# A two-layer hybrid encoder step on one core: the HGRN2 products inside chunks put into one step per group, and a convolution without its zero columns

## The chip, the core and the metric

The program runs on one NeuronCore of one Trainium2 chip. A core has TensorE (PE in the profile; its weight loads are listed apart as PEld), VectorE (DVE), ScalarE (ACT), GpSimd (POOL) and SyncE (SP), which here only issues DMAs. Each engine takes its instructions in the order in which they were written; the engines wait for one another by semaphores. The metric is the device time of one launch in microseconds: the median over runs, 2416.27 us for the kernel before (three runs, 2414.19 to 2416.79).

## The reference

Each of two layers computes `x + W_out . concat[mLSTM | retention | SSD | HGRN2](RMSNorm(x) W_in)` for 1024 prompt frames and 8 streams of 16 frames, 1152 tokens in all, in float32. Two mixers matter here. HGRN2 is a recurrence with a forget decay of its own for every key channel; inside a chunk the score of query t and key s has the decay between them in it, channel by channel:

```python
def hgrn_block(s_prev, xs):
    q, k, v, lf = xs
    b = jnp.cumsum(lf, axis=2)
    diff = b[:, :, :, None, :] - b[:, :, None, :, :]
    w = jnp.exp(jnp.where(causal_tril(l)[:, :, None], diff, -jnp.inf))
    s = jnp.einsum("bhtk,bhsk,bhtsk->bhts", q, k, w)
    o = jnp.einsum("bhts,bhsv->bhtv", s, v) + jnp.einsum("bhtk,bhkv->bhtv", q * jnp.exp(b), s_prev)
    bl = b[:, :, -1]
    s_new = jnp.exp(bl)[..., None] * s_prev + jnp.einsum("bhsk,bhsv->bhkv", k * jnp.exp(bl[:, :, None, :] - b), v)
    return s_new, o
```

The SSD branch begins with a causal depthwise convolution of four taps over the frames (`up = concat([buf, u])`, with a `buf` of three rows that is zero for the prompt), then SiLU. The mLSTM mixer multiplies queries and keys of two heads at a time, masked by head.

## The kernel before

**Work units.** Both layers go through the list `ORDER`: HGRN2 head 0, retention pair 0, SSD half 0, mLSTM pair 0, then h1, r1, s1, m1, h2, h3. A unit has a *projection* (columns of W_in against all 1152 normalised tokens) and a *mixer* (the recurrence). After the units of a layer come two halves of the output projection. The projection is float32 work made of three passes (high part times high part, and each high part times the other's low part), in `slab_run`: lines 404 to 406 where a run gives features on the partitions ("fm": 128 weight columns are held, 384 tokens streamed) and lines 425 to 427 where it gives tokens on the partitions ("tm": 128 tokens are held, 256 weight columns streamed). Three such matmuls, for one of eight blocks of 128 inputs, are called a *k-step* here.

**Interleaving.** `merge` writes the projection of a unit and the mixer of the unit before it into one stream: after each k-step it lets the mixer generator run until its next `yield` (a *step*) when `j * np_ * pace < i * nm_`, where i counts k-steps, j steps, `np_` is the number of k-steps and `nm_` the declared number of steps. So the steps are spread evenly: a mixer with fewer steps has longer ones. A retention projection has 216 k-steps, an HGRN2 projection 120 (72 in its first run, `ev_vg`, and 48 in its second, `ev_qf`). Beside h3's projection runs h2's mixer, of which the last six steps are carried into the output projection (`CARRY`). `self.after(1, f)` runs f at the start of the next step; `self.later(n, f)` runs it n half-chunks of the projection later (`tick`).

**An HGRN2 mixer (`unit_h`, lines 1419 to 1760).** 1152 tokens are nine chunks of 128 in three groups of three. Scores inside a chunk are built from blocks of 4 tokens (`base`, line 1555) and five *levels* of halves of 64, 32, 16, 8 and 4 tokens. `level` makes for each level a tile X of decayed keys and queries: two subtractions on DVE, an exponential on ACT, then, one step later, a product on POOL and one on DVE. `pick` multiplies the halves of X on PE: line 1573 for the three small levels (12 matmuls each with 32-column weights; the profile counts 24 instructions, since a float32 matmul is issued twice), line 1585 for the two large ones (6 matmuls of 32 columns, 3 of 64). Each of base and the five picks has a step of its own and a PSUM tile of its own, evicted in the next step by DVE (`copy_predicated` under a mask, or a copy) or ACT. Level X is made three steps ahead (`LOOK`), and the first two levels of the first group stand in the mixer's opening steps. `prep` makes the decayed keys K and queries Q for the state, `keys` transposes K (line 1605), `state` multiplies K and values (line 1624), `out` forms the outputs (lines 1663, 1665), `post` normalises them (line 1683) and `fin` transposes them back (line 1692). Projection results come in through `ev_qf`; at the next tick `fours` rescales q and k. A mixer has 31 steps for h0 and h1, 29 for h2 and h3.

**Convolution (`unit_s`, `conv`).** A tile of 3 + 384 columns holds the channel's frames; for the first group POOL writes zeros into the three columns ahead (line 1179), and three `scalar_tensor_tensor` operations on DVE (line 1197) add the taps.

**mLSTM (`unit_m`).** At its start the mixer loads decay rows (`load_e`, `load_wi`), multiplies them with the queries on POOL (`use_wi`), then masks the queries by head on POOL (`Z`, through `by_head`), which line 833 multiplies.

Of the kernel before, what the change touches and what calls it, by code (L numbers as in the profile page):

```python
# [120 lines left out]
class Kernel:  # L121
# [609 lines left out]
    def unit_m(self, l, p):  # L731
# [38 lines left out]
        def mix():  # L770
# [175 lines left out]

            load_e(0)
            load_wi(0)
            use_wi(0)
            Z(0)  # L950
# [197 lines left out]
    def unit_s(self, l, u):  # L1148
# [22 lines left out]
        def conv(a, g, ps):  # L1171
# [19 lines left out]
            areas = [(o[:, 0:np_], lambda w: t[:, w:w + np_])]  # L1191
            if g == 2:
                areas.append((o[:, 256:384].rearrange("p (n t) -> p n t", t=16), lambda w: sv[:, :, w:w + 16]))

            def taps(w):
                for oo, src in areas:
                    nc.vector.scalar_tensor_tensor(out=oo, in0=src(w), scalar=cw(w), in1=oo, op0=ALU.mult, op1=ALU.add)
# [221 lines left out]
    def unit_h(self, l, h):  # L1419
# [3 lines left out]
        def ev_qf(m, g, ps):  # L1423
# [30 lines left out]
            self.later(1, lambda: fours(g))  # L1454

# [40 lines left out]
        def mix():  # L1496
            hw = self.vB[:, 40 + 4 * l + h:40 + 4 * l + h + 1]
            stt = {}
            LOOK = 3
# [6 lines left out]

            def level(W, g, li):
                hs = 64 >> li
                w = G3 if (g < 2 or hs <= 8) else 256
                X = self.f()  # L1510
                W["X"][li] = X, w
                xv = lambda a: a[:, 0:w].rearrange("p (n e t) -> p n e t", e=2, t=hs)
                ref = xv(b[g])[:, :, 0, hs - 1:hs].to_broadcast([128, w // (2 * hs), hs])
                self.tt(xv(X)[:, :, 0], ref, xv(b[g])[:, :, 0], ALU.subtract)
                self.tt(xv(X)[:, :, 1], xv(b[g])[:, :, 1], ref, ALU.subtract)
                self.act(X[:, 0:w], X[:, 0:w], AF.Exp)

                def mults():
                    self.tt(xv(X)[:, :, 0], xv(X)[:, :, 0], xv(k[g])[:, :, 0], ALU.mult, "p")
                    self.tt(xv(X)[:, :, 1], xv(X)[:, :, 1], xv(q[g])[:, :, 1], ALU.mult)  # L1520

                self.after(1, mults)
# [24 lines left out]
            def base(g, W):  # L1547


                sc = self.ps("sc")  # L1550
                for c in range(3):
                    for j in range(4):
                        rs = slice(32 * j, 32 * j + 32)
                        ts = slice(128 * c + 32 * j, 128 * c + 32 * j + 32)
                        nc.tensor.matmul(sc[rs, 32 * c:32 * c + 32], k[g][:, ts], q[g][:, ts], start=True, stop=True)
# [3 lines left out]
                self.after(1, lambda: nc.vector.copy_predicated(D, self.lev[:, LEVW - 96:], sc[:, 0:96]))  # L1559

            def pick(g, W, li):
                hs = 64 >> li
                x, w = W["X"].pop(li)
                n = w // 128
                sc = self.ps("sc")
                half = lambda a: a.rearrange("p (n e t) -> p n e t", e=2, t=hs)[:, :, 1]
                if li >= 2:
                    D = W["D"]
                    for c in range(n):
                        for j in range(4):  # L1570
                            rs = slice(32 * j, 32 * j + 32)
                            xt = x[:, 128 * c + 32 * j:128 * c + 32 * j + 32]
                            nc.tensor.matmul(sc[rs, 16 * c:16 * c + 16].rearrange("p (n t) -> p n t", t=hs), xt, half(xt),
                                             start=True, stop=True)
                    cp = lambda a: a.rearrange("p (n t) -> p n t", t=hs)
                    mk = self.lev[:, 48 * (li - 2):48 * (li - 2) + 16 * n]
# [445 lines left out]
```

## Time and profile before

| what | value |
|---|---|
| median of three runs | 2416.27 us |
| the profiled execution | 2415.16 us, its span 2413.4 us |
| PE busy | 2333.9 us (97%), weight loads 2258.8 us |
| DVE, ACT, POOL busy | 1390.7, 1076.4, 976.2 us |
| mean granted TensorE clock | 0.988 |
| DMA | 204.06 MB, mean 85 GB/s |

The span runs from the program's first instruction to its last; 1.8 us of the execution lie outside it. Busy is the time in which an engine has at least one instruction in work. The matmuls overlap, each lasting longer than the distance to the next, so PE's cost is read from the distances between starts. The profile gives the granted clock as a share of full speed (1.00 is 2.4 GHz, 0.50 is 1.2 GHz).

### The profile page before, as it was taken

To read this page: it belongs to the slowest core of one execution; us is meant where nothing else is said; L and a number is where in the kernel's file an instruction comes from. 1 tells how busy PE (TensorE), PEld (TensorE's weight loads), DVE (VectorE), ACT (ScalarE), POOL (GpSimd) and SP (SyncE) were. 2 spreads that over 40 slices of the span, in tenths; PEclk is the share of its full clock that TensorE was granted. 3 is DMA by queue.
4 is the path that set the end of the run, shared out by engine and by line. 5 is a ranking of instruction groups with operands and counts; after the bars stand their busy time and mean duration, and the time that the engine had idled before them with its cause. 6 is when DMAs were issued, how large, how long until landed. Compare 5 with 4: busy or idle time off the path is not lost.

```text
span 2413.4 us, 49607 instructions
## 1 busy us (share of the span) xinstructions
PE 2333.9 (97%) x18992; PEld 2258.8 (94%) x18992; DVE 1390.7 (58%) x3419; ACT 1076.4 (45%) x2780; POOL 976.2 (40%) x1179
## 2 busy tenths in 40 slices
PE   7999999999999998999989999999999999999998
PEld 7999999999999998899988999999899999888998
DVE  4756753773765376544368376537737654666443
ACT  6344563434455345433243445634344653454332
POOL 2443344353334335423135334432633452345353
PEclk9999999999999999999989999999999999999999
DMA  5111233221123222536411212323111333225552
GB/s 151 37 49 45 81 91 77 65 60 52 50 83 95 61 72 74 158 114 213 133 37 37 61 54 80 90 65 77 49 48 55 98 78 81 50 85 167 159 170 82
DMA packets 273736, 204.06 MB, mean 85 GB/s; under 512 B 57908, under 2 KB 264140, under 8 KB 273500
## 3 DMA queue, kind: packets, MB, share of 16 engines
q1 hardware_dynamic: 273180, 200.81, 29.2%
q8 instruction: 150, 2.46, 0.4%
q14 instruction: 86, 0.70, 0.1%
q0 software_dynamic: 320, 0.09, 0.0%
HBM read 148.53 MB, written 52.29 MB: 83 GB/s over the span
## 4 chain that ended last, share of the span: by engine, by line
PE 83%; DVE 8%; ACT 3%; issue 2%; DMA 1%; POOL 1%; SPq 1%; DVEq 0%; ACTq 0%; POOLq 0%
PE w L425 11%; PE w L404 11%; PE w L427 11%; PE w L426 11%; PE w L406 11%; PE w L405 11%; DVE f L212 3%; ACT f L215 2%; PE w L1310 1%; SPq L218 1%; DVE c L212 1%; PE w L1624 1%; PE w L1663 1%; PE w L1061 1%; PE w L833 1%
## 5 line engine op out<-in xcount | busy, mean ns | idle before, releaser
L425 PE MATMUL w<-hi,hnh 128*128 128x256 f32 (+1 forms) x2592 | 775.8, 299 | 0.0
L427 PE MATMUL w<-hi,hnl 128*128 128x256 f32 (+1 forms) x2592 | 731.9, 282 | 1.6 <-DVE hnl L492 1.6
L426 PE MATMUL w<-lo,hnh 128*128 128x256 f32 (+1 forms) x2592 | 731.7, 282 | 0.1
L425 PEld LDWEIGHTS w<-hi,hnh 128*128 128x128 f32 x2592 | 493.0, 190 | 6.1 <-issue 1.1
L426 PEld LDWEIGHTS w<-lo,hnh 128*128 128x128 f32 x2592 | 493.1, 190 | 3.5 <-issue 0.3
L427 PEld LDWEIGHTS w<-hi,hnl 128*128 128x128 f32 x2592 | 492.5, 190 | 2.2 <-DVE hnl L492 2.0
L215 ACT ACTIVATE f<-f 128x384 f32<-128x384 f32 (+1 forms) x475 | 244.1, 516 | 434.8 <-DVE f L212 275.0
L215 ACT ACTIVATE c<-c 128x512 f32<-128x512 f32 (+3 forms) x398 | 211.3, 534 | 292.4 <-DVE c L546 205.4
L212 POOL TENSOR_TENSOR f<-f,f 128x384 f32<-128x384 f32 (+2 forms) x268 | 226.7, 854 | 283.3 <-ACT f L215 210.3
L404 PE MATMUL w<-hnh,hi 128*128 128x384 f32 x960 | 339.3, 353 | 0.0
L212 POOL TENSOR_TENSOR lo<-raw,hi 128x512 fp32r<-128x512 f32 x148 | 195.0, 1318 | 332.3 <-ACT hi L202 279.2
L406 PE MATMUL w<-hnh,lo 128*128 128x384 f32 x960 | 324.6, 338 | 0.0
L405 PE MATMUL w<-hnl,hi 128*128 128x384 f32 x960 | 324.3, 338 | 0.0
L404 PE MATMUL w<-mxh,hi 128*128 128x384 f32 x768 | 268.7, 350 | 0.0
L406 PE MATMUL w<-mxh,lo 128*128 128x384 f32 x768 | 261.1, 340 | 0.0
L405 PE MATMUL w<-mxl,hi 128*128 128x384 f32 x768 | 260.9, 340 | 0.0
L212 POOL TENSOR_TENSOR c<-c,c 128x512 f32<-128x512 f32 (+2 forms) x120 | 128.9, 1083 | 221.2 <-ACT c L215 175.6
L212 DVE TENSOR_TENSOR lo<-raw,hi 128x512 fp32r<-128x512 f32 x140 | 114.4, 817 | 134.4 <-ACT hi L202 134.2
L404 PEld LDWEIGHTS w<-hnh,hi 128*128 128x128 f32 x960 | 181.6, 189 | 3.0 <-issue 1.8
L405 PEld LDWEIGHTS w<-hnl,hi 128*128 128x128 f32 x960 | 181.8, 189 | 0.8
L406 PEld LDWEIGHTS w<-hnh,lo 128*128 128x128 f32 x960 | 181.0, 189 | 0.0
L212 DVE TENSOR_TENSOR c<-c,w 128x384 f32<-128x384 f32 (+1 forms) x124 | 73.3, 595 | 184.8 <-PE w L406 121.6
(304 smaller groups left out, 3979.3 us busy)
## 6 DMA issues: line engine op xcount, KB each, us to landing
raw<-in_w_in SPq DMA_DIRECT2D x224, 128.0 KB
raw<-in_w_in SPq DMA_DIRECT2D x112, 256.0 KB
c<-mixd SPq DMA_DIRECT2D x96, 192.0 KB
raw<-in_w_out SPq DMA_DIRECT2D x64, 256.0 KB
xd<-c SPq DMA_DIRECT2D x66, 192.0 KB
mixd<-c SPq DMA_DIRECT2D x48, 256.0 KB
c<-xd SPq DMA_DIRECT2D x60, 192.0 KB
c<-sscr SPq DMA_DIRECT2D x36, 256.0 KB
```

Of the source, the lines that this page charges most:

```text
L212: (self.nc.vector if e == "v" else self.nc.gpsimd).tensor_tensor(out=out, in0=a, in1=b, op=op)
L215: self.nc.scalar.activation(out=out, in_=in_, func=func, scale=scale, bias=bias, **k)
L218: (e or self.nc.sync).dma_start(out=out, in_=in_)
L404: nc.tensor.matmul(o, hi[:, k, ms], xhi[:, k, :], start=(k == 0), stop=False)
L405: nc.tensor.matmul(o, hi[:, k, ms], xlo[:, k, :], start=False, stop=False)
L406: nc.tensor.matmul(o, lo[:, k, ms], xhi[:, k, :], start=False, stop=(k == KT - 1))
L425: nc.tensor.matmul(o, xhi[:, k, ts], hi[:, k, :w], start=(k == 0), stop=False)
L426: nc.tensor.matmul(o, xhi[:, k, ts], lo[:, k, :w], start=False, stop=False)
L427: nc.tensor.matmul(o, xlo[:, k, ts], hi[:, k, :w], start=False, stop=(k == KT - 1))
L833: nc.tensor.matmul(sc[:, 0:256], k[g][:, cs], qz.pop(c), start=True, stop=True)
L1061: nc.tensor.matmul(po[h], w[:, h], v[j][:, i, h], start=(c in (0, 8)), stop=(c == 0 or (c < 8 and h == 1)))
L1310: nc.tensor.matmul(po[:, 64 * h:64 * h + 64], pt[:, h], x_[:, 64 * h:64 * h + 64], start=True, stop=True)
```

## The change

**HGRN2.** The step functions `base` and `pick` are gone. `gram` issues all 57 products of a group in one step: 12 of base, 36 of the small levels, then 6 and 3 of the two large ones, into two PSUM tiles. One step later `evac` evicts all of them and builds the diagonal blocks (`diag`). `level` has moved out of the mixer. The first group's five levels are put off with `later` from `ev_qf`, so that they stand beside the unit's own projection; the levels of group g + 1 stand in the first three of the five steps of group g, `prep(g + 1)` in the third, `fresh(g + 1)` (the two POOL memsets) in the fourth. The mixer has 24 steps for every head: one opening step (`prep` and `fresh` of the first group), fifteen, and eight at the end. No DMA is added or taken away.

**Convolution.** The memset is gone; for the first group each tap covers only the columns that exist.

**mLSTM.** `Z(0)` stands ahead of `load_e(0)`, `load_wi(0)` and `use_wi(0)`.

```diff
@@ unit_m, mix
+            Z(0)
             load_e(0)
             load_wi(0)
             use_wi(0)
-            Z(0)
@@ unit_s, conv
-            if g == 0:
-                nc.gpsimd.memset(t[:, 0:3], 0.0)
-            else:
+            if g > 0:
...
+            if g == 0:
+                areas = [((lambda w: o[:, 3 - w:np_]), lambda w: t[:, 3:w + np_])]
@@ unit_h, ev_qf
             self.later(1, lambda: fours(g))
+            if g == 0:
+                for li in range(NLEV):
+                    self.later(2 + li, lambda li=li: level(Ws[0], 0, li, self.later))
@@ unit_h, mix
+            def gram(g, W):
+                sc, sb = self.ps("sc"), self.ps("sc")
+                mm = lambda o, a, b_: nc.tensor.matmul(o, a, b_, start=True, stop=True)
+                at = lambda li: 96 + 48 * (li - 2)
+                for c in range(3):
+                    for j in range(4):
+                        ts = slice(128 * c + 32 * j, 128 * c + 32 * j + 32)
+                        mm(sc[32 * j:32 * j + 32, 32 * c:32 * c + 32], k[g][:, ts], q[g][:, ts])
+                for li in range(2, NLEV):
+                    hs = 64 >> li
+                    x, w = W["X"].pop(li)
+                    for c in range(n):
+                        for j in range(4):
+                            xt = x[:, 128 * c + 32 * j:128 * c + 32 * j + 32]
+                            o = sc[32 * j:32 * j + 32, at(li) + 16 * c:at(li) + 16 * c + 16]
+                            mm(o.rearrange("p (n t) -> p n t", t=hs), xt, half(xt, hs))
+                for li in (1, 0):
...
+                            mm(sb[64 * j:64 * j + hs, 192 * li + hs * c:192 * li + hs * c + hs], xt[:, 0:hs], xt[:, hs:2 * hs])
+                def evac():
+                    nc.vector.copy_predicated(D, self.lev[:, LEVW - 96:], sc[:, 0:96])
...
+                    diag(W)
+                self.after(1, evac)
...
+            prep(0, Ws[0])
+            fresh(Ws[0])
+            yield
             for g in range(NG):
...
+                for s in range(5):
+                    if s == 0:
+                        gram(g, W)
+                        if V:
+                            out(g - 1, V, 0)
+                    elif s == 1:
                         keys(g, W)
+                        if V:
+                            out(g - 1, V, 1)
+                            out(g - 1, V, 2)
+                    elif s == 2 and V:
+                        post(g - 1, V)
+                    elif s == 3:
                         state(g, W)
...
+                    elif s == 4 and V:
+                        fin(g - 1, V)
+                    if g + 1 < NG:
+                        for li in ((0, 1), (2, 3), (4,), (), ())[s]:
+                            level(Ws[g + 1], g + 1, li, self.after)
+                        if s == 2:
+                            prep(g + 1, Ws[g + 1])
+                        if s == 3:
+                            fresh(Ws[g + 1])
                     yield
-        ... steps=31 if h < 2 else 29 ...
+        ... steps=24 ...
```

On PE, the first group of the first HGRN2 unit of layer 0 stood in the kernel before in six places with projection matmuls between them; four of the six are shown (w is a PSUM tile, f a tile of 384 columns, hi and lo weights, hnh and hnl tokens; sizes are those of the result, partitions by columns).

```order
L427 MATMUL w_1185<-hi_794,hnl_232 128x256
L1555 MATMUL w_1195<-f_792,f_827 32x32 x12
L425 MATMUL w_1185<-hi_794,hnh_231 128x256
...
L427 MATMUL w_1185<-hi_794,hnl_232 128x256
L1585 MATMUL w_1264<-f_1098 64x64 x3
L425 MATMUL w_1185<-hi_794,hnh_231 128x256
...
L1585 MATMUL w_1309<-f_1134 32x32 x6
L1605 MATMUL w_1320<-cst,f_1213 128x128 x3
L425 MATMUL w_1302<-hi_794,hnh_301 128x256
...
L1573 MATMUL w_1351<-f_1218 32x16 x12
```

Now the same products stand in one piece:

```order
L427 MATMUL w_1064<-hi_794,hnl_159 128x256
L1562 MATMUL w_1122<-f_792,f_827 32x32 x12
L1562 MATMUL w_1122<-f_907 32x16 x12
L1562 MATMUL w_1122<-f_943 32x16 x12
L1562 MATMUL w_1122<-f_984 32x16 x12
L1562 MATMUL w_1123<-f_888 32x32 x6
L1562 MATMUL w_1123<-f_866 64x64 x3
L425 MATMUL w_1064<-hi_794,hnh_158 128x256
L426 MATMUL w_1064<-lo_795,hnh_158 128x256
```

The products themselves, their number and their shapes are the same; the projection matmuls that stood between them now stand before and after.

On DVE, beside that unit's own second projection run, the next thing after `fours` of the first group (lines 1464 and 1469) was the eviction of the next group:

```order
L1464 SCALAR_TENSOR_TENSOR f_844<-t_843,f_825 128x384
L1469 TENSOR_SCALAR f_825<-t_843 128x384
L546 TENSOR_SCALAR f_909<-w_884 128x384
L1436 SCALAR_TENSOR_TENSOR f_911<-f_911,oml,f_910 128x384
```

Now (lines 1486 and 1491) the subtractions and DVE's products of the first levels follow it:

```order
L1486 SCALAR_TENSOR_TENSOR f_844<-t_843,f_825 128x384
L1491 TENSOR_SCALAR f_825<-t_843 128x384
L212 TENSOR_TENSOR f_866<-f_825 128x3x64 x2
L212 TENSOR_TENSOR f_888<-f_825 128x6x32 x2
L212 TENSOR_TENSOR f_866<-f_866,f_792 128x3x64
L212 TENSOR_TENSOR f_907<-f_825 128x12x16 x2
L212 TENSOR_TENSOR f_888<-f_888,f_792 128x6x32
L546 TENSOR_SCALAR f_925<-w_894 128x384
```

The subtractions and products of the first group have moved from the steps beside the next unit's projection to this place; the other two levels follow behind the next eviction.

On POOL, at the start of the first mLSTM mixer, the decay product (which needs a DMA) stood ahead of the masked queries:

```order
L777 MEMSET mC_5075 128x258
L212 TENSOR_TENSOR f_5079<-f_5079,f_4912 128x384
L212 TENSOR_TENSOR t_5085<-f_4912,cst 128x256
L212 TENSOR_TENSOR t_5110<-f_4912,cst 128x256
L212 TENSOR_TENSOR t_5133<-f_4912,cst 128x256
```

Now the first masked queries (t from f and the constants cst) stand ahead of it:

```order
L777 MEMSET mC_5047 128x258
L212 TENSOR_TENSOR t_5049<-f_4884,cst 128x256
L212 TENSOR_TENSOR f_5053<-f_5053,f_4884 128x384
L212 TENSOR_TENSOR t_5082<-f_4884,cst 128x256
L212 TENSOR_TENSOR t_5105<-f_4884,cst 128x256
```

The masked queries of the first chunk moved past the decay product, and the others stay behind it.

## Rows read from the trace of the kernel before

**Rows 1.** The page, part 1: busy time, share of the span and instructions.

```profile
PE 2333.9 (97%) x18992; PEld 2258.8 (94%) x18992; DVE 1390.7 (58%) x3419; ACT 1076.4 (45%) x2780; POOL 976.2 (40%) x1179
```

**Rows 2.** Waits of PE: line waited for, releaser: us in total, times, longest.

```profile
PE w L1605 <- DVE f L212: 10.0, 8, 2.4
PE w L1692 <- DVE f L1683: 8.3, 3, 3.1
PE w L1045 <- POOL c L1179: 7.9, 4, 2.0
PE w L1585 <- POOL f L212: 7.0, 4, 3.2
PE w L833 <- POOL t L212: 3.7, 4, 0.9
```

**Rows 3.** Timeline of PE around three bursts: start, us, engine, line, operation.

```profile
114.67 0.28 PE L426 MATMUL w<-lo,hnh 128*128 128x256 f32 x1
114.78 0.28 PE L427 MATMUL w<-hi,hnl 128*128 128x256 f32 x1
115.00 0.38 PE L1573 MATMUL w<-f 128*32 128x16 f32 x24
115.31 0.38 PE L425 MATMUL w<-hi,hnh 128*128 128x256 f32 x1
...
156.29 0.28 PE L427 MATMUL w<-hi,hnl 128*128 128x256 f32 x1
156.49 0.32 PE L1573 MATMUL w<-f 128*32 128x16 f32 x16
156.74 0.39 PE L425 MATMUL w<-hi,hnh 128*128 128x256 f32 x1
...
186.95 0.28 PE L427 MATMUL w<-hi,hnl 128*128 128x256 f32 x1
187.06 0.49 PE L1692 MATMUL w<-cst,f 128*128 128x128 f32 x3
187.31 0.37 PE L425 MATMUL w<-hi,hnh 128*128 128x256 f32 x1
```

**Rows 4.** Windows, PE alone, first-group stretches of six units: us, busy, clock, DMA.

```profile
sum 78.80, PE 55.97; mean PE 9.33
```

**Rows 5.** Windows: us, PE, PEld, DVE, ACT, POOL busy, PEclk, DMA, GB/s.

```profile
110.30:113.70 3.40, 3.00 (x14) 3.03 (x15) 3.40 (x7) 1.05 (x2) 1.78 (x2) 0.50 0.28 84
902.20:905.60 3.40, 3.40 (x27) 3.17 (x26) 2.85 (x4) 1.97 (x6) 2.79 (x4) 0.50 0.01 2
2096.90:2107.10 10.20, 8.48 (x50) 8.01 (x51) 7.52 (x16) 5.17 (x12) 6.51 (x10) 0.50 0.09 28
```

**Rows 6.** Timeline of POOL as the first mLSTM mixer starts.

```profile
420.23 1.04 POOL L212 TENSOR_TENSOR f<-f,f 128x384 f32<-128x384 f32 x1 [10.61 <-DVE s L205]
```

**Rows 7.** Timeline of POOL, then of PE, in the first retention mixer.

```profile
201.52 0.61 POOL L212 TENSOR_TENSOR t<-t,cst 128x256 f32<-128x256 f32 x1
202.07 0.10 POOL L1179 MEMSET c<- 128x3 f32 x1
...
202.19 0.57 PE L1045 MATMUL w<-t,t 128*128 128x256 f32 x1 [1.97 <-POOL c L1179]
```

**Rows 8.** Windows: second HGRN2 unit's projection (end), third unit's mixer beside the fourth's.

```profile
467.00:492.00 25.00, 25.00 (x194) 23.97 (x193) 19.22 (x56) 9.99 (x32) 8.79 (x12) 1.00 0.33 79
918.00:942.00 24.00, 22.60 (x291) 20.40 (x290) 19.17 (x57) 12.98 (x39) 9.58 (x17) 1.00 0.17 53
```

**Rows 9.** Lines of DVE by form (count, busy, mean ns), then timeline of DVE twice.

```profile
L212 DVE TENSOR_TENSOR f<-f 128x192 f32<-128x192 f32 x208 | 110.9, 573 | 0.0
L212 DVE TENSOR_TENSOR f<-f,f 128x192 f32<-128x192 f32 x104 | 51.3, 494 | 22.4 <-ACT f L215 21.9
...
1292.65 0.61 DVE L212 TENSOR_TENSOR f<-f 128x192 f32<-128x192 f32 x2
...
1297.82 1.70 DVE L212 TENSOR_TENSOR f<-f 128x192 f32<-128x192 f32 x2
```

More of the change, by code (lines that the diff above doesn't have):

```diff
@@ L1454, in ev_qf, with level, mults @@
             self.later(1, lambda: fours(g))
+            if g == 0:
+                for li in range(NLEV):
+                    self.later(2 + li, lambda li=li: level(Ws[0], 0, li, self.later))
+        Ws = [{"X": {}} for _ in range(NG)]
+        def level(W, g, li, put_off):
+            hs = 64 >> li
+            w = G3 if (g < 2 or hs <= 8) else 256
+            X = self.f()
+            W["X"][li] = X, w
+            xv = lambda a: a[:, 0:w].rearrange("p (n e t) -> p n e t", e=2, t=hs)
+            ref = xv(b[g])[:, :, 0, hs - 1:hs].to_broadcast([128, w // (2 * hs), hs])
+            self.tt(xv(X)[:, :, 0], ref, xv(b[g])[:, :, 0], ALU.subtract)
+            self.tt(xv(X)[:, :, 1], xv(b[g])[:, :, 1], ref, ALU.subtract)
+            self.act(X[:, 0:w], X[:, 0:w], AF.Exp)
+            def mults():
+                self.tt(xv(X)[:, :, 0], xv(X)[:, :, 0], xv(k[g])[:, :, 0], ALU.mult, "p")
+                self.tt(xv(X)[:, :, 1], xv(X)[:, :, 1], xv(q[g])[:, :, 1], ALU.mult)
+            put_off(1, mults)
         def fours(g):
@@ L1505, in load_states @@
                     stt[j] = t
[L1507 to L1522, printed above, removed]
             sv = lambda a, n=3: a[:, 0:128 * n].rearrange("p (c t) -> p c t", t=128)
@@ L1545, in prep, with fresh @@
                 self.after(1, mults)
[L1547 to L1555, printed above, removed]
+            def fresh(W):
                 W["ST"], W["D"] = ST, D = self.f(), self.t(96)
@@ L1569, in pick @@
                     for c in range(n):
                         for j in range(4):
-                            rs = slice(32 * j, 32 * j + 32)
                             xt = x[:, 128 * c + 32 * j:128 * c + 32 * j + 32]
[L1573 to L1576, printed above, removed]
@@ L1577, in pick @@
-                    self.after(1, lambda: nc.vector.copy_predicated(half(D[:, 0:32 * n]), cp(mk), cp(sc[:, 0:16 * n])))
-                    if li == NLEV - 1:
-                        self.after(1, lambda: diag(W))
-                    return
-                for c in range(n):
-                    for j in range(64 // hs):
-                        rs = slice(64 * j, 64 * j + hs)
-                        xt = x[:, 128 * c + 64 * j:128 * c + 64 * j + 2 * hs]
-                        nc.tensor.matmul(sc[rs, hs * c:hs * c + hs], xt[:, 0:hs], xt[:, hs:2 * hs], start=True, stop=True)
@@ L1727, in mix @@
                             load_states()
-                    if g > 0:
-                        V = Ws[g - 1]
-                        for cc in {0: (0,), 1: (1, 2)}.get(li, ()):
-                            out(g - 1, V, cc)
-                        if li == 2:
-                            post(g - 1, V)
-                        if li == 4:
-                            fin(g - 1, V)
-                            Ws[g - 1] = None
+                    elif s == 4 and V:
+                        fin(g - 1, V)
+                        Ws[g - 1] = None
+                    if g + 1 < NG:
[5 more added lines that the diff above has]
+                            fresh(Ws[g + 1])
                     yield
@@ L1753, in mix @@
             yield
-        return dict(runs=[("tm", ev_vg), ("fm", ev_qf)], mix=mix, steps=31 if h < 2 else 29, gate=(lambda: self.gate_prep(l, gt)) if h == 0 else None)
+        return dict(runs=[("tm", ev_vg), ("fm", ev_qf)], mix=mix, steps=24, gate=(lambda: self.gate_prep(l, gt)) if h == 0 else None)
     def mix_load(self, l, half, g):
```

63 lines of the change are left out of this document (25 added, 38 removed).

## The prediction

> **What bounds the kernel now.** I read the page first. PE is busy for 97% of the span and no other engine for more than 58% [rows 1]. So the time is PE's work, plus the 79 us (2413.4 less 2333.9) in which it idles, plus what it loses at the lower clock; an edit on another engine counts only through these. The second view is PE's own waits [rows 2]: of those that the change touches, lines 1605, 1692, 1585 and 833 make 29 us. The third is PE's timeline, read from one projection matmul to the next, since a busy PE is not a PE at its peak [rows 3]. There the distance between two plain projection matmuls is about 0.12 us (114.67 to 114.78).
>
> **One step instead of six: the visits.** From the end of the projection matmul before a burst to the end of the one behind it, less one plain distance, is what the burst costs. Twelve products of a small level (24 instructions): (115.31 + 0.38) - (114.78 + 0.28) - 0.12 = 0.51 us. Eight (16 instructions): (156.74 + 0.39) - (156.29 + 0.28) - 0.12 = 0.44 us. So 8 instructions cost 0.07 us and 24 of them 0.21, and 0.30 us is paid for the visit itself. Three transposes over the full array: (187.31 + 0.37) - (186.95 + 0.28) - 0.12 = 0.33 us, 0.11 each, about their own length; a visit there costs nothing [rows 3]. So the 0.30 belongs to going from 128-column weights to narrow ones and back. Before, a group goes there six times; now once. The products cost the same in either place. Five visits times 0.30 is 1.50 us per group; there are 24 groups (two layers, four heads, three groups).
>
> Inside the new step the weights change from 32 to 64 columns once. None of the rows has such a change. It costs between nothing and another 0.30; I take 0.15, the middle, for lack of a nearer row. That leaves 1.35 us times 24 = **32 us** (29 to 36).
>
> The Trainium skill, "TensorEngine Tiling (Array Packing)", section "Key Properties", says that a change of tiling mode drains the engine. Rows 3 agree for the way in and out (0.30 us); by that rule the step from 32 to 64 columns drains too, the term would be 24 x 1.20 = 29 us and the time 3 us more.
>
> **The first group's waits.** When a mixer starts, its first levels and `prep` are made in the opening steps and PE runs into them: lines 1585 (7.0), 1605 (10.0) [rows 2], and smaller ones at 1573 and 1624. The six stretches in which this happens have 78.80 - 55.97 = 22.8 us of idle PE [rows 4]. In the changed kernel the levels are ready before the mixer begins, so lines 1585 and 1573 have nothing to wait for. The transposes of `keys` still stand two steps behind `prep`, but steps are longer: beside a retention projection 216/24 = 9.0 k-steps against 216/31 = 7.0. A k-step is three plain distances, 0.36 us; two steps give 6.5 us where they gave 5.0, and the one large burst between them adds about another 0.6. The longest wait was 2.4 us [rows 2]; 0.3 of it is left, and on h0 some more, because DVE has the gates' scan between K's subtraction and product. I take **20 us** of the 22.8 (12 to 22.8).
>
> PE's clock comes with it. In three stretches in those starts the granted clock was 0.50, that is 1.2 GHz, after PE had stood waiting; in them it was busy 3.00, 3.40 and 8.48 us [rows 5]. At 2.4 GHz the same work takes half: **7.4 us** back if all three go (3 if one stays and is longer).
>
> **The last group's transposes.** `fin` waits for line 1683, 8.3 us in three waits [rows 2]. Two steps lie between `post` and `fin` before and after; beside h3's projection a step grows from 120 x 0.9 / 23 = 4.7 to 120 x 0.9 / 18 = 6.0 k-steps, 0.9 us over two. DVE is in order there, and the evictions of h3's projection stand ahead of the scaling. I take **5 us** (0 to 8.3).
>
> **The masked queries.** POOL idled 10.61 us behind the wait of the decay product for its DMA, with `by_head` queued behind it [rows 6], and line 833 waited 3.7 us in four mixers [rows 2]. With `Z(0)` ahead, POOL does it in the idle time: **3.7 us** (2 to 3.7). `use_wi` starts 0.6 us later at most, before its DMA has landed.
>
> **The zero columns.** The wait at line 1045, 7.9 us, is put down to the memset [rows 2]. The timeline says otherwise: `by_head` runs from 201.52 to 202.13, the memset ends at 202.17, the matmul starts at 202.19 [rows 7]. It needs the masked queries; the memset is only the last event nearby, and `by_head` waits for the product ahead of it, which stays. So the edit is worth 16 times 0.1 us on an engine with room: **nothing**, and the 7.9 us stay. The taps lose six columns of 1152 per tile: nothing.
>
> **What is added.** Nothing new is computed, and no DMA moves past a queue except that the sample states are loaded one level later, a whole group ahead of their use. But ten subtractions and five DVE products per unit move from the mixer's start to the unit's own second projection run: 10 x 0.573 + 5 x 0.494 = 8.2 us at their mean [rows 9]. That run is 25 us long with DVE busy for 19.22 [rows 8]: 27.4 of 25. Beside it runs an mLSTM mixer (h1, h2) or h2's mixer (h3), whose DVE work is queued behind the new one and which PE then waits for; six runs in all. The subtractions took 0.30 each where POOL had nothing else to do and 0.85 beside a POOL product [rows 9]. In the run POOL is busy for 8.79 of 25 us, so the true demand lies between 4.7 us (ten at 0.30, five at 0.34) and 8.2.
>
> The Trainium skill, "SBUF — State Buffer", section "Who interferes with whom", says that a VectorE instruction with two SBUF inputs blocks against a GpSimd instruction that reads SBUF. The 0.30 and 0.85 agree. By it the move to a stretch where POOL works less makes the levels cheaper, the loss below would be nothing and the time 10 us less.
>
> Evictions also come in one piece: nine DVE operations and two on ACT, some 2 us, with four steps until `out` needs them. The levels of group g + 1 have two whole steps until `gram`. Where h2's mixer runs beside h3's projection, DVE was already busy for 19.17 of 24 us [rows 8], and the same work must fit a stretch that PE would leave some 10 us sooner. I charge 1.7 us to each of the six runs, **10 us** (0 to 30, the latter if every run loses 5).
>
> **Sum.** 32 + 20 + 7.4 + 5 + 3.7 - 10 = 58 us. The profiled execution took 2415.16 us (span 2413.4 and 1.8 around it): 2357. It was 1.1 us under the median of the runs shown, so 2358 is forecast.
>
> **Rivals.**
> *The waits move, and only the visits pay.* DVE in order speaks for it: what PE no longer waits for at a mixer's start, it waits for in the run where DVE is full. Against it: over the span DVE is busy for 58%. Then 32 us: 2384. Chance 0.17.
> *A visit has no price of its own.* If the 0.30 us is the first products' own start-up and each kind of product pays it again inside the step, merging saves nothing on PE; 26 us remain (58 less 32): 2390. For it: the large and the small products differ in shape. Against it: 16 instructions cost nearly as much as 24 [rows 3]. Chance 0.08.
> *Slower: DVE becomes the bound in the HGRN2 projections.* Demand there is 27.4 of 25 us, and DVE also stands still while ACT forms the gate exponentials. If PE waits 7.5 us in each of six runs and then runs on at 1.2 GHz, losing up to 4.2 (half of the 8.48) each time, it costs 70 us, against 68 gained: 2418, and up to 2430 if the runs lose 2 us more. It decides from 11 us per run. Chance 0.05.
> *Nothing to be measured* (within 0.2%, 5 us, about what a measurement of this kernel can tell from no change): the same with less. Chance 0.03.
> *More than forecast*: every wait goes, no new one comes, 32 to 64 is free: 36 + 22.8 + 7.4 + 8.3 + 3.7 = 78, or 2338. That lies in the range; below 2330 only if a visit costs more than rows 3 show. Chance 0.05.
> The forecast itself, 2330 to 2380, has 0.62.
>
> **Range and chances.** 2330 to 2395 holds the forecast, the first two rivals and the ends of the unknown terms (28.8 + 12 + 3 + 0 + 2 - 30 = 16 would be 2400, all at once unlikely). Faster 0.92, same 0.03, slower 0.05.
>
> **What would show it.** PE's instructions of the new step lie in one burst of some 1.7 to 1.9 us, and PE's busy time falls by about 32 us, and by 7 more with the clock. The waits at the products disappear from PE's list, that of `keys` falls below 3 us in total, line 833's disappears, line 1045's stays near 7.9 under another name. DVE's busy share in the second run of h1's projection rises from 0.77 to 0.95 or more; new waits of PE there, in mLSTM lines, are the 10 us. I am wrong if the bursts of the new step take over 2.5 us, or if PE's idle time does not fall.

## The result, and the profile after

The changed kernel is slower: 2435.3 us, median of four runs (2434.61 to 2436.16), against 2415.6 for the kernel before on the same chip; ratio 1.0082 (95% interval 1.0064 to 1.0099). 2358 was forecast. The profiled execution has a span of 2434.4 us, 21.0 more than before. Page, part 1 [rows 1]:

```profile
PE 2320.9 (95%) x18992; PEld 2267.5 (93%) x18992; DVE 1375.8 (57%) x3371; ACT 1069.8 (44%) x2764; POOL 955.3 (39%) x1147
```

Read as in the prediction, PE's time has three parts. PE's idle time (span less busy) rose from 79.5 to 113.5 us. Within the span the trace's record of the granted clock has 57 us at 0.50 before and 106 after (the mean clocks give 2 x (1 - 0.988) x 2413 = 58 and 2 x (1 - 0.978) x 2434 = 107, the same within their rounding); PE was busy in 49.6 and 84.1 us of it, and lost half of that, 24.8 and 42.1. PE's work, counted at full clock, fell from 2309.1 to 2278.8. So 34.0 + 17.3 - 30.3 = 21.0 us: **the work saved is there, and idling and the lower clock took it back with interest.** Waits of PE, columns as in [rows 2]:

```profile
PE w L1634 <- ACT f L202: 20.4, 7, 5.9
PE w L1615 <- DVE f L212: 15.5, 5, 6.5
PE w L1866 <- DMA c<-in_x_prompt: 14.3, 2, 9.0
PE w L1562 <- POOL f L212: 12.9, 11, 3.7
...
PE w L1045 <- POOL t L212: 7.8, 4, 2.0
PE w L404 <- ACT mxh L202: 4.7, 2, 3.9
...
PE w L1562 <- DVE f L212: 3.9, 2, 2.8
PE w L405 <- POOL mxl L212: 2.2, 2, 1.8
...
PE w L1702 <- DVE f L1693: 0.9, 1, 0.9
```

Of the same list before, what [rows 2] has not:

```profile
PE w L1859 <- DMA c<-in_x_prompt: 4.8, 2, 3.1
PE w L1573 <- POOL f L212: 3.8, 4, 1.2
...
PE w L1624 <- ACT f L202: 3.7, 6, 0.7
```

Line 1634 is `state` (3.7 before), 1615 `keys` (1605 before), 1562 `gram` (1573 and 1585 before, 10.8 together), 1866 the transposes of the layer input x (1859 before, 4.8), 404 and 405 the output projection (none before), 1702 `fin`. Line 833 is gone; 1045 stands at 7.8 and is now put down to the masked queries, as was read from [rows 7].

It goes wrong in the same place at all six mixer starts beside a projection (h0, h1 and h2 of each layer). The end of h1's projection and the last scan (line 1445) of its third group, before, then the first products:

```profile
492.31 0.33 PE L406 MATMUL w<-hnh,lo 128*128 128x384 f32 x1
...
496.53 0.40 DVE L1445 TENSOR_TENSOR_SCAN f<-cst,f 128x128 f32<-128x128 f32 x1
...
505.00 0.40 PE L1555 MATMUL w<-f,f 128*32 128x32 f32 x24
```

and after:

```profile
491.78 0.33 PE L406 MATMUL w<-hnh,lo 128*128 128x384 f32 x1
...
491.94 1.02 DVE L212 TENSOR_TENSOR f<-f 128x192 f32<-128x192 f32 x2
...
494.47 0.62 DVE L212 TENSOR_TENSOR f<-f 128x192 f32<-128x192 f32 x2
...
495.59 0.40 PE L1562 MATMUL w<-f,f 128*32 128x32 f32 x24
...
498.79 0.62 DVE L1436 SCALAR_TENSOR_TENSOR f<-f,oml,f 128x384 f32<-128x384 f32 x1 [1.82 <-ACT f L215]
...
500.37 0.40 DVE L1445 TENSOR_TENSOR_SCAN f<-cst,f 128x128 f32<-128x128 f32 x1
```

Two things moved against each other. DVE ends the projection's own third group 8.7 us behind PE's last projection matmul (500.77 less 492.11) instead of 4.3, since the first group's levels now stand ahead of it: the subtractions of the last two (491.94 and 494.47) begin only as the projection ends. And the mixer wants its first products 3.5 us behind that matmul instead of 12.4, since the opening steps are gone. What the first two groups need of DVE is then queued behind this. DVE, PE and ACT some 10 us on:

```profile
504.34 2.78 DVE L212 TENSOR_TENSOR f<-f 128x192 f32<-128x192 f32 x4
504.56 0.52 PE L1615 MATMUL w<-cst,f 128*128 128x128 f32 x3
...
508.52 0.70 DVE L1594 COPY_PREDICATED t<-lev,w 128x48 f32<-128x48 uint8 x3
...
509.40 1.01 DVE L205 COPY f<-t 32x96 f32<-32x96 f32 x4
...
510.42 1.95 DVE L212 TENSOR_TENSOR f<-f,f 128x192 f32<-128x192 f32 x2
512.29 1.94 DVE L212 TENSOR_TENSOR f<-f 128x192 f32<-128x192 f32 x4
513.72 1.06 ACT L215 ACTIVATE f<-f 128x384 f32<-128x384 f32 x2 [3.64 <-DVE f L212]
...
515.33 0.49 ACT L202 ACTIVATE f<-w 128x384 f32<-128x384 f32 x1
...
515.87 1.44 PE L1634 MATMUL w<-c,f 128*128 128x128 f32 x6 [4.40 <-ACT f L202]
```

ACT's copy of the transposed keys (515.33) needs only the transposes, which were through at 505.08, but ACT takes its work in order, and ahead of it stand exponentials of the second group's levels, for which ACT has waited 3.64 us. PE names ACT; ACT names DVE. Far from there, where h3's projection ends and the output projection begins, a late DVE reaches a DMA queue:

```profile
979.03 0.67 DVE L212 TENSOR_TENSOR lo<-raw,hi 128x512 fp32r<-128x512 f32 x1
979.72 0.38 SPq L218 DMA_DIRECT2D raw<-in_w_out  x1
980.20 2.79 SPq L218 DMA_DIRECT2D c<-mixd  x6
983.08 2.88 SPq L218 DMA_DIRECT2D c<-in_x_prompt  x6
...
987.02 1.35 PE L1866 MATMUL w<-cst,c 128*128 128x128 f32 x5 [9.04 <-DMA c<-in_x_prompt]
```

SP reloads `raw` only when DVE has read it, and the loads of x stand behind that on SP (the first of them issued at 971.06 before, at 983.08 now).

### The profile page after: what moved, and what is told of

It reads as the page before. It is cut to its first block, busy times and chain, and to the rows that moved or that the text cites. A ratio compares the mean times of both kernels' runs of the same rounds, so it can differ in the third digit from the quotient of the medians.

```text
span 2434.4 us, 49366 instructions
## 1 busy us (share of the span) xinstructions
PE 2320.9 (95%) x18992; PEld 2267.5 (93%) x18992; DVE 1375.8 (57%) x3371; ACT 1069.8 (44%) x2764; POOL 955.3 (39%) x1147
## 4 chain that ended last, share of the span: by engine, by line
PE 78%; DVE 12%; ACT 5%; issue 2%; DMA 1%; POOL 1%; SPq 0%; ACTq 0%; DVEq 0%; POOLq 0%
PE w L425 12%; PE w L427 11%; PE w L426 11%; PE w L404 9%; PE w L406 9%; PE w L405 9%; ACT f L215 3%; DVE f L212 3%; PE w L1310 1%; PE w L1562 1%; DVE f L1445 1%; PE w L1673 1%; PE w L1634 1%; DVE c L212 1%; PE w L1061 1%
## 5 line engine op out<-in xcount | busy, mean ns | idle before, releaser
L425 PEld LDWEIGHTS w<-hi,hnh 128*128 128x128 f32 x2592 | 498.9, 192 | 4.9 <-issue 1.1
L426 PEld LDWEIGHTS w<-lo,hnh 128*128 128x128 f32 x2592 | 498.4, 192 | 3.4 <-issue 0.3
L215 ACT ACTIVATE f<-f 128x384 f32<-128x384 f32 (+1 forms) x459 | 232.2, 516 | 341.2 <-DVE f L212 187.9
L212 POOL TENSOR_TENSOR f<-f,f 128x384 f32<-128x384 f32 (+2 forms) x252 | 213.4, 863 | 222.1 <-ACT f L215 152.2
```

The source lines that it names most:

```text
L212: (self.nc.vector if e == "v" else self.nc.gpsimd).tensor_tensor(out=out, in0=a, in1=b, op=op)
L215: self.nc.scalar.activation(out=out, in_=in_, func=func, scale=scale, bias=bias, **k)
L425: nc.tensor.matmul(o, xhi[:, k, ts], hi[:, k, :w], start=(k == 0), stop=False)
L426: nc.tensor.matmul(o, xhi[:, k, ts], lo[:, k, :w], start=False, stop=False)
```

## The experiments

Times are medians, ratios to the kernel before as run beside each.

### The parts of the change, each alone

**Small edits** (kernel before, with `Z(0)` moved and the convolution's edit, nothing else).


> The kernel before with the two small edits alone: the masked queries of the first chunk ahead of the decay product, and the convolution without zero columns. Theory (the loss comes from where the HGRN2 levels stand on VectorE): line 833's wait of 3.7 us goes, line 1045's 7.9 us stay, some 2412 us. Rival (the small edits cost something, by VectorE's odd widths or a changed order on GpSimd): 2420 us or more.


Measured 2409.4 us, 0.9977 (0.9967 to 0.9986): the theory, by 2.6 us more than its figure. Line 833's wait is gone and line 1045's 7.9 us stay. That the gain is this wait is not shown: in the profile PE idles as long as before (79.7 and 79.5 us), other waits having grown, and what fell is the loss at the lower clock (15.4 and 24.8).

**One step for the products** (kernel before with `gram` in the sixth step of a group; all else, the levels' timetable too, as before).

```diff
-                        base(g, W)
                         prep(g, W)
-                    else:
-                        pick(g, W, li)
+                    elif li == 3:
+                        fresh(W)
+                    elif li == 4:
+                        gram(g, W)
```

> The kernel before with the 57 products of a group in one step (its sixth), everything else in the old timetable: levels three steps ahead, one a step, the first group's in the mixer's opening steps. Theory (the visits pay, and the loss is made by the timetable of the levels): 24 visits instead of 144 give 30 us, and the waits at the first products (10.8 us) go, 2375 to 2390 us. Rival (the eviction in one lump is what hurts, whatever the levels do): the wait at the state products rises as it did, from 3.7 to some 20 us, and the time is 2405 us or more.


Measured 2398.9, 0.9934 (0.992 to 0.9949): between theory and rival. PE's work at full clock is 2282.2, 26.9 us less, so the visits pay nearly what was forecast; but PE idles 13.3 us more, above all for the first group's keys:

```profile
PE w L1611 <- DVE f L212: 24.7, 8, 7.6
```

**Both together.**


> The kernel before with the products merged into the sixth step of a group and with the small edits (Z first, convolution without zero columns), old timetable of the levels. If the two add up: 2399 - 5 = 2392 to 2396 us, ratio about 0.991, and L1045's waits of 7.9 us are still there while L833's 3.7 are gone. If the small edits only pay where DVE is idle, 2399 or more.


Measured 2397.6, 0.9926 (0.9906 to 0.9946): between the two figures, nearer to the second; the intervals overlap too far to tell whether the small edits still pay here. The burst of the new step can be read in it alone:

```profile
516.69 0.28 PE L427 MATMUL w<-hi,hnl 128*128 128x256 f32 x1
516.90 0.40 PE L1558 MATMUL w<-f,f 128*32 128x32 f32 x24
517.11 1.56 PE L1558 MATMUL w<-f 128*32 128x16 f32 x90
518.60 0.39 PE L425 MATMUL w<-hi,hnh 128*128 128x256 f32 x1
```

(518.60 + 0.39) - (516.69 + 0.28) - 0.12 = 1.90 us for 114 instructions, where 1.7 to 1.9 was forecast.

**The early levels alone** (kernel before, products still in six steps; the first group's five levels beside its own projection).

```diff
+            if g == 0:
+                for li in range(NLEV):
+                    self.later(2 + li, lambda li=li: level(Ws[0], 0, li, self.later))
```

> The kernel before with one thing moved: the first group's five levels stand beside the unit's own projection; the products keep their six steps. Theory (that place makes VectorE late, and the split of the weights and the loads of the input behind it): the waits at the transposes of the input rise from 4.8 to 12 us or more, waits at the first products do not go, 2425 to 2440 us. Rival (the place is harmless, the lump of the merged step does it): the first products no longer wait, 2400 to 2412 us.


Measured 2439.4, 1.0102 (1.0087 to 1.0117): this part alone costs 25 us, as the theory had it. But the waits at the first products, which were to stay (10.8), are gone, and those for x came to 10.3 where 12 or more was expected. Its waits are for the first group's keys, for the gates' scan and for x:

```profile
PE w L1610 <- DVE f L212: 23.6, 6, 7.4
PE w L1862 <- DMA c<-in_x_prompt: 10.3, 2, 7.1
...
PE w L638 <- DVE c L630: 5.3, 2, 3.9
```

### Where the changed kernel waits

**First group's levels back in the mixer** (changed kernel; the five levels in five opening steps, 29 steps).

```diff
+            for li in range(NLEV):
+                level(Ws[0], 0, li, self.after)
+                yield
             prep(0, Ws[0])
```

> The changed kernel with the first group's five levels back in the mixer, one in each of five opening steps, 29 steps in all; products in one step, two levels a step for the later groups. Theory: the waits at the transposes of the input fall back to about 5 us, those at the first products to under 5; the waits at the state products (20 us) stay, since two levels a step and the eviction in a lump stay: 2395 to 2412 us. Rival (the lump and the short timetable make all of the loss): 2425 us or more.


Measured 2427.3, 1.0056 (1.0039 to 1.0073): the rival's time, though not by its way. The late x loads (5.0) and `keys` (none) are cured as the theory said, and `state`, which was to stay at 20, fell to 9.7; but the products, which were to wait under 5 us, now wait for most of it:

```profile
PE w L1559 <- POOL f L212: 47.3, 16, 7.1
PE w L1631 <- ACT f L202: 9.7, 5, 2.7
```

The last level's POOL product is wanted two steps behind its subtractions, where the kernel before had three.

**Less work on DVE, first group** (changed kernel; the first group's ten subtractions per unit left out, the exponentials read the scan: part of the computation is missing).

```diff
+            if g > 0:
-            self.tt(xv(X)[:, :, 0], ref, xv(b[g])[:, :, 0], ALU.subtract)
+                self.tt(xv(X)[:, :, 0], ref, xv(b[g])[:, :, 0], ALU.subtract)
...
+            self.act(X[:, 0:w], (X if g > 0 else b[g])[:, 0:w], AF.Exp)
```

> The changed kernel without the ten subtractions of the first group's levels (the exponentials read the scan directly; part of the computation is left out), so some 5 us of DVE less in each of the six HGRN2 projections, in its second run. Theory: DVE lag in that run makes the late flips (14.3 us), the late mxh/mxl (6.9) and a part of the first keys (12.3 of 15.5): these fall to 5, 2 and 5, the time falls by 12 to 25 us to 2410 to 2423; the state's 20.4 stay. Rival: these waits come from the mixer's own order: 2430 to 2436.


Measured 2412.7, 0.9993 (0.9979 to 1.0007), 22.6 us under the changed kernel: the price of the early levels is the ten subtractions. The edit takes away two things at once, DVE's time for them and the exponentials' wait for them, and no run parts the two. The gain is not all where I said: the products recover (16.8 to 4.5), x (the "flips") in part (14.3 to 8.8), the output projection's inputs (mxh and mxl, lines 404 and 405) from 6.9 to 4.6, and `keys` gets worse:

```profile
PE w L1616 <- DVE f L212: 21.8, 6, 6.8
PE w L1635 <- ACT f L202: 20.2, 7, 5.9
...
PE w L1867 <- DMA c<-in_x_prompt: 8.8, 2, 6.6
...
PE w L1563 <- POOL f L212: 4.5, 10, 1.3
```

**The eviction in two steps** (the copies into the big matrix one step behind the masked ones).

```diff
                 self.after(1, evac)
+                self.after(2, rest)
```

> The changed kernel with the eviction of the products in two steps (the masked copies in the step behind the products, the copies into the big matrix one step later). Theory: the waits for the state (20.4 us, ACT's transposed keys queued behind two exponentials whose inputs stand behind the eviction on DVE) fall to 10 or less, time 2420 to 2428 us. Rival: the state waits because DVE is behind for other reasons (levels two a step, first group): state waits stay at 17 or more and the time stays within 2432 to 2438.


Measured 2443.1, 1.0114 (1.0095 to 1.0133); `state` waits 27.5 us. The theory fell, and the time is above the rival's too: the piece on DVE was not too large in one step.

**The next group's levels over four steps.**

```diff
-                        for li in ((0, 1), (2, 3), (4,), (), ())[s]:
+                        for li in ((0, 1), (2,), (3,), (4,), ())[s]:
```

> The changed kernel with the next group's levels begun two, one, one, one in four steps instead of two, two, one in three. Theory: the state waits 20.4 us because ACT's copy of the transposed keys is queued behind the exponentials of two levels, whose inputs DVE makes late; with one level there the state waits 10 us or less, the time falls by 8 to 16 to 2419 to 2428. Rival: DVE is late whatever the order (its whole work in the first two groups is the cause): state 16 or more, or the products gain what it loses: 2431 to 2440.


Measured 2440.7, 1.0102 (1.0085 to 1.0119); `state` 17.3, products 21.2. The rival holds: with one exponential less ahead of the keys' copy, PE waits about as long.

**No subtractions at all** (as above, in all groups).


> The changed kernel with the subtractions of all levels of all groups left out (the exponentials read the scan directly; part of the computation is left out): 272 DVE operations fewer, 128 us of DVE, 5.3 us in each of 24 groups. Leaving out the first group's alone gave 2412.7 with the waits for the state still at 20.2 us and for the keys at 21.8. Theory (DVE's amount of work beside the first two groups is what waits there, in whatever place): state and keys together fall from 42 to under 15 us and the time to 2375 to 2395. Rival (the order of the steps, ACT's queue above all, makes them wait): they stay at 30 or more, the time at 2405 to 2413.


Measured 2391.7, 0.9903 (0.989 to 0.9917):

```profile
PE w L1612 <- DVE f L212: 23.6, 6, 7.8
...
PE w L1631 <- ACT f L202: 2.1, 4, 1.0
```

`state` falls to 2.1: in the order as it stands it waited for the subtractions of the second group's levels (for DVE's time or, again, for their place ahead of the exponentials). `keys` does not fall, so theory and rival each get one half; that the first group's keys wait because of where the mixer begins is an argument from this, not shown.

**Two empty steps ahead of the first products** (changed kernel, 26 steps).

```diff
             fresh(Ws[0])
             yield
+            yield
+            yield
```

> The changed kernel with two empty steps between the first group's preparation and its products (26 steps in place of 24). Theory: the changed mixer begins its first group two to four steps sooner after the projection's last group than the kernel before, and meets that group's own chain of gate, scan and exponentials, which DVE works off in order and waits for ACT in between; two steps more let it pass: products 16.8 and keys 15.5 us of waits fall to 5 each, the time to 2412 to 2422 (the late flips and the state's waits stay). Rival (the amount of DVE work decides, wherever the steps lie): the waits move to the state and the time stays within 2428 to 2438.


Measured 2419.0, 1.0017 (1.0008 to 1.0026): 16.3 us back by doing nothing, and within the theory's figure. The products' wait goes (0.8); that of `keys` stays (16.6), against the expectation, and `state` rises to 26.6:

```profile
PE w L1634 <- ACT f L202: 26.6, 8, 7.4
PE w L1615 <- DVE f L212: 16.6, 4, 6.3
```

**Both remedies: levels in the opening steps and two empty steps** (31 steps, as before the change).


> The changed kernel with the first group's levels back in the mixer's five opening steps (2427.3 us, products waiting 48.9) and two empty steps more between the preparation and the products: 31 steps, as many as the kernel before. Theory: what the new mixer lacks is slack between the first group's last level (its POOL product stands behind the other mixer's work) and the products; with it products wait 8 us or less and the time is 2400 to 2412, still above the 2397.6 of the old timetable with the same products, as two levels a step load DVE in the second group. Rival (the waits only move to the state and keys, over 45 us together): 2418 to 2428.


Measured **2393.6, 0.9913 (0.9897 to 0.993)**, faster than theory and rival said. PE idles 86.6 us and its work is 2280.0. Of h1's start:

```profile
489.97 0.33 PE L406 MATMUL w<-hnh,lo 128*128 128x384 f32 x1
...
494.19 0.40 DVE L1445 TENSOR_TENSOR_SCAN f<-cst,f 128x128 f32<-128x128 f32 x1
...
510.12 0.40 PE L1559 MATMUL w<-f,f 128*32 128x32 f32 x24
```

DVE is through 4.3 us behind the projection again, and the first products come 19.8 us behind it. The products still wait 26.5 us in all (8 were expected), `state` 8.8, `keys` not at all. The levels are as dense here as in the changed kernel, two in a step, so that density, which I had taken for a part of the loss, costs no time that shows against the kernel of both parts (one level a step, 2397.6) once the mixer starts in time. Of the 26.5 us, 3.5 stand in second groups, where that kernel has no wait at the products.

### Searching for a better order of the old timetable

**Products a step earlier, keys and state a step later**, from the kernel of both parts together, then **keys and state a step later alone** (only the last two lines).

```diff
-                    elif li == 3:
+                    elif li == 2:
                         fresh(W)
-                    elif li == 4:
+                    elif li == 3:
                         gram(g, W)
...
-                    if li == 1:
+                    if li == 2:
                         keys(g, W)
-                    if li == 3:
+                    if li == 4:
                         state(g, W)
```

> As the run with merge and small edits, but the products one step earlier (fourth of the levels' steps in place of the fifth), so that their evictions no longer share a step with the next group's preparation, and keys and state each one step later. Theory: the keys' wait of 24.7 us in the merged kernel is the first group's preparation on a DVE that is behind; one step more gives it room: keys to 5 us or less, 2370 to 2382 us. Rival: DVE is behind for the whole first group, so what the keys win the products or the outputs lose again: 2388 to 2398.

> The merged kernel with the small edits, with keys and state one step later each and the products where they were (sixth step). Theory (first group late on DVE by less than two steps): keys under 8 us, products under 5, 2380 to 2390 us. Rival (the outputs, which need the state's update two steps behind, wait in their place, or the products do): 2394 to 2402.


The first: 2399.7, 0.9935 (0.9915 to 0.9956), `keys` 12.3, but products 21.1. The second: 2394.1, 0.9911 (0.9895 to 0.9926), `keys` 12.2, products 5.4, but `state` 19.0. The rival in the first, 1.7 us past its range; the second ends on the rival's edge, and it was `state` that waited in place of the keys, which neither side had named.

**Preparation a step earlier** (from both parts together), and from the kernel with keys and state later **two more opening steps for h2 and h3** and **diagonal copies on ACT**:

```diff
             level(Ws[0], 0, 1)
-            for _ in range(2 if h < 2 else 2):
-                yield
+            yield
+            prep(0, Ws[0])
+            yield
...
-                        prep(g, W)
+                        if g > 0:
+                            prep(g, W)
...
-            for _ in range(2 if h < 2 else 0):
+            for _ in range(2):
...
-DG = "v"
+DG = "a"
```

> The merged kernel with the small edits (2397.6 us), with the first group's preparation one step earlier, in the empty step ahead of its first levels' end. Theory: the first keys (24.2 us of waits, 20 of them in the first group) wait because their factor's multiplication stands on DVE behind the third level; moved ahead of it, keys fall to 10 us or less and the time to 2380 to 2390 us. Rival: DVE is simply full over the first group, so the waits move to products, state or outputs: 2394 to 2400.

> The merged kernel with the small edits and with keys and state one step later (2394 us), with the third and fourth head's mixers opened by the same two empty steps as the first two heads' (31 steps in place of 29). In that kernel the longest waits for keys stand in just those mixers (4.6 and 5.8 us, in the others 1.3 and less). Theory: these go, 2383 to 2390 us. Rival (a shorter pace of the steps takes it back, or DVE is as late two steps on): 2391 to 2398.

> The merged kernel with the small edits and with keys and state one step later (2394 us), with the four diagonal copies of a group on ACT in place of DVE: 96 DVE operations of 242 ns less, 1.9 us in the first two groups of each of 8 mixers, as many on ACT. Theory (DVE's work bounds the opening of each mixer): up to 1.9 x 8 = 15 us less, some half of it behind other work: 2382 to 2391. Rival (ACT is as late as DVE there, and the transposed keys wait behind the new copies): 2393 to 2402.


2399.9, 0.9936 (0.9921 to 0.995), with `keys` down to 12.6 and `state` up to 22.5; 2395.9, 0.9921 (0.9907 to 0.9934); 2400.2, 0.9941 (0.9928 to 0.9955). Three times the rival: in this timetable a wait taken from one line of PE appears at another. These kernels lie within 6 us of one another; the best of them and the one with both remedies cannot be told apart, and both beat the kernel before by some 20 us and the changed one by 41.

## Why the prediction was wrong, point by point

**Visits (32 us): right in the mechanism, some 2 to 6 us too much.** PE's work at full clock fell by 30.3 us in the changed kernel, by 26.3 to 30.2 in the other kernels with merged products; that is 1.10 to 1.26 us per group, 0.22 to 0.25 per visit saved. The Trainium skill, "TensorEngine Tiling (Array Packing)", section "Key Properties", by which the change from 32 to 64 columns drains as well, would have had 29. The runs lie nearer to that than to 32, but none has the change from 32 to 64 columns by itself. That a visit has no price of its own, the second rival, is ruled out.

**The first group's waits (20 us): the step that failed.** The prediction said that "the levels are ready before the mixer begins, so lines 1585 and 1573 have nothing to wait for". It counted how long each step becomes and not how many are gone ahead of the first products. Levels made sooner meet products wanted 8.9 us sooner (at h1); these wait 16.8 us instead of 10.8. With the opening steps left in place, in the run of the early levels alone, the products indeed had nothing to wait for. For `keys` a longest wait of 0.3 us and less than 3 us in total were forecast; they are 6.5 and 15.5. `state`, 3.7 before, was taken for a small part of this term: 20.4. And PE's idle time, which had to fall if the prediction was right, rose by 34 us. The four kernels with and without two remedies:

| | levels beside the own projection | in the opening steps |
|---|---|---|
| products at once | 2435.3 (the changed kernel) | 2427.3 |
| two empty steps first | 2419.0 | 2393.6 |

Either remedy alone gives 8 or 16 us, both give 42, more than the two added. The 16.3 us in the left column measure missing steps: only their number differs there. The columns differ in more than the place, since the levels bring five opening steps of their own; levels beside the projection with seven empty steps were not run. The parts agree with it: the merged products with the small edits won 15.5 us and the early levels alone lost 24.8, which would make 9 us slower. The changed kernel is 20 slower; if parts can be added, the rest is what no part alone has, the short timetable.

**Added (10 us, bounds 0 to 30): mis-sized.** The early levels cost 25 us by themselves, with the opening steps still there, and 22.6 come back without their subtractions. In the mLSTM lines, where the 10 us were looked for, PE waits little more than before (line 891: 3.9 us, 1.8 before). I had asked how full DVE is in the second run; its share there hardly rose (19.36 us of 25, against 19.22 in [rows 8]), and the 0.95 that was to show the overload never came. What counts is the queue: the third group's chain, with DVE waiting for ACT in between, ends 4.4 us later in h1, and all of the mixer behind it. The Trainium skill, "SBUF — State Buffer", section "Who interferes with whom", fits the operations: in the trace before, 104 subtractions of 192 columns with no `TENSOR_TENSOR` of POOL beside them took 0.35 us in the mean, 104 with one 0.80. In the changed kernel 116 of 192 have none, and the mean is 494 ns instead of 573 [rows 9]; DVE's products of that size went the other way, from 494 to 560. The conclusion that the loss would then be nothing was wrong. Nor was the 0.30 in [rows 9] read rightly as one beside an idle POOL, which had two products in work:

```profile
1292.53 2.02 POOL L212 TENSOR_TENSOR c<-c,c 128x256 f32<-128x256 f32 x2 [2.40 <-DVE c L212]
```

**Clock (7.4 us back): wrong sign.** PE still stands waiting in the mixer starts, and 17.3 us more were lost at 1.2 GHz; from 493 to 520 us, h1's start, the mean granted clock is 0.87, 1.00 before.

**The last group's transposes (5 us): right in size.** 8.3 became 0.9; with 26 steps 1.8, with 29 and 31 again 9.0 and 9.2, so the longer steps do it, as argued. They are not the only way: with keys and state a step later, 3.5 us were left at h2's 29 steps.

**Masked queries, zero columns: right in the waits.** Line 833's 3.7 us are gone, nothing is gained at line 1045; as a run of their own the two edits gave 5.2 us, of which the profile does not show how much is that wait.

**The rivals.** The one on the slower side named the engine (DVE) and nearly the time (2418 to 2430), but not the path: DVE was not full in the projections, and at 25 us over six starts the early levels stayed far under its 11 us per run. The time came out so because the 20 us of gain it was set against were not there.

**Open.** Why thinning the first group's levels leaves `keys` waiting longer (21.8 against 15.5) was only read in part. The longest waits are h0's, where the gates' scan stands on DVE between K's subtraction and its product, but they hardly change (6.5 and 5.8 us in the changed kernel, 5.2 and 6.8 without the subtractions). All of the growth is at h1 and h2, where the products wait less: there products and keys together have 13.8 and 11.7 us, so most of it is one wait under another name. What the keys wait for then, no run singles out. And of the last kernel's 26.5 us of products no run tells whether a third empty step would end them.

## What to carry to other kernels

When work is moved ahead of the point that needs it, check that the point has not moved too: compare, in the changed order, the distance from the last producer in the engine's queue to the first consumer, not the number of instructions in front of one of them. Empty-looking steps at the start of a pipeline can be what covers the tail of the stage before; take them out last, and measure that alone. And a mean busy share of 0.77 says nothing on how late an in-order engine is when part of its queue waits for another engine.

## What the runs showed that I had not expected

- The same lateness goes by several names: DVE's appeared as ACT's at `state`, as POOL's at the products and as a DMA's, 9.04 us, at the input transposes.
- Idling can cost more than itself: here 34 us more of it came with 49 us more at the granted clock of 0.50, in which another 17 us were lost. It is no fixed price: with both parts together PE idled 91.2 us and lost 19.8 at that clock, with keys and state later 83.1 and 30.4.
